# A feed-forward's last projection with Strassen's scheme on 7 of its 20 pairs of weight rows

## The chip, the cores and the metric

The kernel runs on one core of a Trainium2 chip. The core has a matrix engine (TensorE, PE in the profile; PEld is its loading of the stationary operand), a vector engine (VectorE, DVE), a scalar engine (ScalarE, ACT), a general engine (GpSimd, POOL) and an engine whose queue issues transfers here (SyncE, SP). Each engine works through its own list of instructions and waits at semaphores for the others. Data lie in SBUF (128 partitions), products in the 8 banks of PSUM (128 x 512 fp32 each).

The metric is device time in microseconds, the median of several executions. A separate profiled execution gives the trace.

## The reference

A decoder trunk of two layers for 256 tokens of width 2048, in fp32. What matters here is the feed-forward and what stands behind it:

```python
def conv_glu(x, w_gate, w_up, conv_w, w_down):
    gate = causal_dwconv(x @ w_gate, conv_w)
    return (jax.nn.silu(gate) * (x @ w_up)) @ w_down
...
        x = layer_norm(DN_ALPHA * x + h, ln1_g[i], ln1_b[i])
        f = conv_glu(x, ffn_w_gate[i], ffn_w_up[i], ffn_conv_w[i], ffn_w_down[i])
        x = layer_norm(DN_ALPHA * x + f, ln2_g[i], ln2_b[i])
        x = x + jax.nn.sigmoid(x @ ple_w_gate[i]) * (p[i] @ ple_w_proj[i])
```

`w_gate` and `w_up` are 2048 x 5120, `w_down` is 5120 x 2048. Layer 0 has a gated delta-rule mixer ahead of this, layer 1 a sparse attention.

## The kernel before

**Splitting.** A matrix product is done in fp32r on TensorE with each operand split in two: a high half (a copy into fp32r on ACT, L127) and a low half (the rest, on DVE, L128). The product is high x high, low x high and high x low, three matmuls. Activations are kept split: `hT` holds the feed-forward's inner activations, transposed, 40 blocks of 128 rows, each with a high and a low plane of 256 tokens (32 blocks in the tile hTA, 8 in hTB). Weights come from HBM into `raw` (4 buffers of 128 x 1024 fp32, issued on SP's queue, L122) and are split into `hi` and `lo` (3 buffers each, 128 x 1024).

**Gate and up.** `ffn` runs over pairs of blocks n, n+1 of the 5120 columns. `gemm_t_steps` (L160, L164) computes the gate and then the up product of a pair, transposed; `gate` applies the convolution and Silu, `up` multiplies the two and splits the result into `hT` (L941 to L943). Both read `xT`, the split transposed input, which nobody needs after the last up product until the layer norm writes it anew.

**The last projection.** `project` computes `hT` x `w_down` in four blocks of 512 columns, one after the other (`project_steps`, `gemm_steps`). A step takes two row-blocks of 128 and 512 columns of weights, one `raw` and one `hi`/`lo`, and does 12 matmuls of 512 columns: for each row-block and each half of 128 tokens, high x high (L199) and low x high (L202), then high x low for all (L206). Two PSUM banks hold the two token halves. At the end of a block `residual` adds the sum to 4^(1/4) times `x` (L263) and takes statistics (L264). That is 20 steps of 12 for each block, 960 matmuls per layer.

**The end.** In the last block the last two steps are taken together, first the whole of token half 0, then of half 1, so that the layer norm's scale of half 0 (`scale_of`, L297 to L306) is worked out while half 1 runs. `held` splits two weight tiles of the next projection ahead of time; `fetch` loads the small projection's weights into the upper half of `xT` ahead of the last block; `fill` runs that small projection (`ple_w_proj`) on TensorE while the layer norm transposes its rows (L331) and writes `xT`.

**Order.** Instructions get a priority by the order in which the code writes them; `high_priority` moves some forward, and the weights' splits stand 1000 places forward. When the program is built, each engine's list is made from these priorities and from what is ready at each point by the builder's own times; `after` pins one instruction behind another. A tile's buffer is free for the next use when its last reader has done.

**PSUM.** The tags `mm0` and `mm1` have two banks each and are taken in turn (`banks`); `sp` and `bk` have two each, for everything else.

## Time and profile before

| | us |
|---|---|
| median of 3 runs | 2766.88 |
| lowest and highest | 2762.75, 2767.78 |
| profiled execution | 2763.9 |
| its span in the profile | 2762.1 |

The profile has one row for each group of alike instructions: its line in the kernel, engine, operation, the names of the tiles (written <- read), the shape, the count; then busy time and the mean of one in ns; then the idle time of the engine ahead of it and what ended it. The view of windows gives the busy time of each engine in a stretch. The view in order of time gives start and length of each instruction or run of alike ones. Ends of matmuls are modelled and overlap the next one's start, so the spacing of the starts is what counts.

### The profile page before, as it was taken

The page shows a single profiled execution, that of the slowest core. Times are in us where ns is not written, and L with a number is a line of the kernel's source. Part 1 is how long each engine was busy: PE and PEld are TensorE (multiplying, and loading weights), DVE is VectorE, ACT ScalarE, POOL GpSimd, SP SyncE. Part 2 cuts the span into 40 slices and gives each one's busy share as a digit, 9 for nine tenths or more (in the row PEclk, how much of TensorE's full clock was granted, in tenths as well). Part 3 has the DMA queues.
Part 4 walks back from the last instruction along what each step waited for, and adds up shares of the span by engine and source line. Part 5 has one row for each costly group of instructions (what it writes and reads, how often), then busy time and mean ns, then how long its engine had stood idle before and what let it go on. Part 6 is the DMA issues. An engine that isn't in the chain of part 4 may idle for free. (4 is left out here: it accounts for less than half of the span.)

```text
span 2762.1 us, 40056 instructions
## 1 busy us (share of the span) xinstructions
PE 2735.3 (99%) x14604; PEld 2352.9 (85%) x14604; DVE 1853.0 (67%) x3109; ACT 1485.7 (54%) x2512; POOL 428.9 (16%) x834
## 2 busy tenths in 40 slices
PE   9999999999999999999999999999999999999999
PEld 7888888888888888888888888888888888888887
DVE  7877877877466666666545765765766666655566
ACT  5576666776545555555334544455455555543444
POOL 1665545665000000000000000210000000000000
PEclk9999999999999999999999999999999999999999
DMA  8776667666575666676666567545566666666655
GB/s 225 188 203 175 181 176 187 157 192 168 187 217 158 193 206 204 204 208 198 196 193 207 176 189 234 170 145 165 167 198 197 199 191 193 197 192 194 209 172 193
DMA packets 410566, 525.09 MB, mean 190 GB/s; under 512 B 24352, under 2 KB 299024, under 8 KB 410112
## 3 DMA queue, kind: packets, MB, share of 16 engines
q1 hardware_dynamic: 397872, 495.65, 59.7%
q0 software_dynamic: 12496, 26.88, 3.9%
q8 instruction: 114, 1.87, 0.3%
q14 instruction: 84, 0.69, 0.1%
HBM read 516.62 MB, written 8.97 MB: 190 GB/s over the span
## 5 line engine op out<-in xcount | busy, mean ns | idle before, releaser
L128 DVE TENSOR_TENSOR lo<-raw,hi 128x1024 fp32r<-128x1024 f32 (+1 forms) x920 | 1125.3, 1225 | 582.1 <-ACT hi L127 565.0
L127 ACT ACTIVATE hi<-raw 128x1024 fp32r<-128x1024 f32 (+1 forms) x920 | 967.1, 1053 | 664.8 <-PE mm_ps L202 415.4
L160 PE MATMUL mm_ps<-xT,hi 128*128 128x512 f32 (+1 forms) x4176 | 1031.8, 395 | 7.6 <-DVE xT L242 5.6
L160 PEld LDWEIGHTS mm_ps<-xT,hi 128*128 128x128 f32 (+1 forms) x4176 | 763.1, 189 | 154.8 <-ACT hi L241 6.1
L164 PE MATMUL mm_ps<-xT,lo 128*128 128x256 f32 (+1 forms) x4176 | 557.0, 284 | 1.7 <-DVE lo L128 1.7
L164 PEld LDWEIGHTS mm_ps<-xT,lo 128*128 128x128 f32 (+1 forms) x4176 | 538.7, 191 | 23.2 <-DVE lo L128 2.5
L199 PE MATMUL mm_ps<-hi,xT 128*128 128x512 f32 (+1 forms) x704 | 272.3, 388 | 0.0
L202 PE MATMUL mm_ps<-hi,xT 128*128 128x512 f32 (+1 forms) x704 | 269.0, 384 | 0.0
L237 ACT ACTIVATE fold<-mm_ps 128x256 f32<-128x256 f32 x261 | 98.0, 376 | 264.7 <-PE mm_ps L160 264.2
L256 POOL DMA_DIRECT2D lng<-in_ln_g x16 | 8.8, 549 | 1239.6 <-PE mm_ps L206 654.0
L202 PE MATMUL mm_ps<-hi,hTA 128*128 128x512 f32 x512 | 199.3, 389 | 0.0
L199 PE MATMUL mm_ps<-hi,hTA 128*128 128x512 f32 x512 | 199.3, 389 | 0.0
L206 PE MATMUL mm_ps<-lo,xT 128*128 128x512 f32 (+1 forms) x704 | 189.4, 384 | 0.0
L202 PEld LDWEIGHTS mm_ps<-hi,xT 128*128 128x128 f32 x704 | 132.3, 188 | 24.4
L199 PEld LDWEIGHTS mm_ps<-hi,xT 128*128 128x128 f32 x704 | 132.2, 188 | 24.1
L206 PEld LDWEIGHTS mm_ps<-lo,xT 128*128 128x128 f32 x704 | 129.8, 188 | 24.3
L206 PE MATMUL mm_ps<-lo,hTA 128*128 128x512 f32 x512 | 136.9, 389 | 0.0
L688 POOL TENSOR_TENSOR xi<-xi,xt 128x60 f32<-128x60 f32 (+24 forms) x248 | 121.2, 489 | 19.4
L686 POOL TENSOR_TENSOR xt<-ld,xi 128x60 f32<-128x60 f32 (+24 forms) x248 | 114.1, 460 | 53.4 <-DMA ld<-lt 34.6
L199 PEld LDWEIGHTS mm_ps<-hi,hTA 128*128 128x128 f32 x512 | 96.1, 188 | 20.0
L206 PEld LDWEIGHTS mm_ps<-lo,hTA 128*128 128x128 f32 x512 | 96.2, 188 | 19.9
L202 PEld LDWEIGHTS mm_ps<-hi,hTA 128*128 128x128 f32 x512 | 96.2, 188 | 19.8
(268 smaller groups left out, 2657.7 us busy)
## 6 DMA issues: line engine op xcount, KB each, us to landing
raw<-in_gdn_w_in SPq DMA_DIRECT2D x192, 512.0 KB, 4.5
raw<-in_ffn_w_gate SPq DMA_DIRECT2D x160, 512.0 KB, 4.1
raw<-in_ffn_w_up SPq DMA_DIRECT2D x160, 512.0 KB, 4.4
raw<-in_ffn_w_down SPq DMA_DIRECT2D x160, 512.0 KB, 3.8
raw<-in_dsa_w_in SPq DMA_DIRECT2D x72, 512.0 KB, 3.7
raw<-in_gdn_w_o SPq DMA_DIRECT2D x64, 512.0 KB, 4.2
raw<-in_ple_w_gate SPq DMA_DIRECT2D x64, 512.0 KB, 4.8
raw<-in_dsa_w_o SPq DMA_DIRECT2D x32, 512.0 KB, 3.8
```

Source lines behind the costliest of these rows:

```text
L127: act = nc.scalar.activation(hi, raw, AF.Copy)
L128: ins = nc.vector.tensor_tensor(lo, raw, hi.bitcast(F32), op=ALU.subtract)
L160: ins = nc.tensor.matmul(q[:m, :], hi[:, k, o:o + m], x[:, k0 + k].rearrange("p a b -> p (a b)"), start=k0 + k == 0, stop=last)
L164: ins = nc.tensor.matmul(q[:m, S:], lo[:, k, o:o + m], x[:, k0 + k, 0, :], start=False, stop=last)
L199: ins = nc.tensor.matmul(ps[a][:, :n], xh, hi, start=k == 0, stop=False)
L202: self.before = self.recent = nc.tensor.matmul(ps[a][:, :n], xl, hi, start=False, stop=False)
L206: self.last = self.recent = nc.tensor.matmul(ps[a][:, :n], x(k)[:, 0, a * P:(a + 1) * P], lo, start=False, stop=k == kt - 1)
L237: nc.scalar.activation(t[:m], ps[:, S:], AF.Copy)
L256: ins = self.nc.gpsimd.dma_start(out=r, in_=bass.AP(tensor=src.tensor, offset=src.offset, ap=[[0, P], [1, n]]))
L686: nc.gpsimd.tensor_tensor(tmp[:, :m, :w], bcast(ld[:, i + 1:, i], m, 1), xi[:, :m, i:i + 1].to_broadcast([P, m, w]), op=ALU.mult)
L688: nc.gpsimd.tensor_tensor(xi[:, :m, i + 1:], xi[:, :m, i + 1:], tmp[:, :m, :w], op=ALU.subtract)
```

## The change

Of the 20 pairs of row-blocks in `w_down` (2m and 2m+1), 7 (m = 0, 3, 6, 9, 12, 15, 18) go by Strassen's scheme. There the left operand is 2 x 2 blocks (two token halves, two row-blocks), the right one 2 x 2 (two row-blocks, two column blocks of 512), and seven products with sums of blocks as operands take the place of eight. I call these the fast pairs and the other 13 the plain ones.

- The projection now goes over two column halves of 1024. A plain pair takes two `raw` tiles, one row-block of 1024 columns each, and does 24 matmuls into four banks. A fast pair takes two such tiles as well and does 21 matmuls into seven banks.
- `pair` makes the right operands: in place in `raw`, four sums of 512 columns on DVE, and splits into two `hi`/`lo` tiles (the first block of the first row-block; both blocks of the second) and into the lower half of `xT`, planes `th` and `tl` (four sums). The order is: split of the first block, two sums, split of the second row-block, two sums, two splits into `xT`.
- The left operands come from `up`: for fast pairs it forms sums of token halves, three forms of 128 columns per pair. For the first two fast pairs they are split into the new tile `some` at once; for the other five they wait as fp32 in free parts of `pw` and are split into the upper half of `xT` just ahead of their first use.
- Three products go straight into the banks of the result (`own`), four into banks of their own (`one`, `six`, `seven`, `five`), which gather over all seven fast pairs. After the last fast pair of a column half (`j == final`) one ACT copy and eight DVE sums of 512 columns add them to `x`; the closing sum (`done`) then is one addition and the statistics for each of four blocks.
- The two column halves use the two sets of four banks in exchange.
- The last pair of the second half finishes token half 0 in two blocks of 512 columns, then half 1 in two. `fetch` comes after the last fast pair.

```diff
--- before.py
+++ after.py
@@ -915,6 +915,168 @@
         return self.layer_norm(pool, g, b, gb, copies)
 
 
+    def pair(self, src, m, c):
+
+
+        nc = self.nc
+        raw = [self.wp.tile([P, 1024], F32, tag="raw", name="raw") for _ in range(2)]
+        for k, r in enumerate(raw):
+            nc.sync.dma_start(out=r, in_=src[(2 * m + k) * P:(2 * m + k + 1) * P, c:c + 1024])
+        flat = self.xT.rearrange("p k a s -> p k (a s)")
+        th, tl = flat[:, 0:4], flat[:, 4:8]
+        (h0, l0), (h1, l1) = ((self.hl.tile([P, 1024], F32R, tag=k, name=k) for k in ("hi", "lo")) for _ in range(2))
+        (b11, b12), (b21, b22) = ((r[:, :512], r[:, 512:]) for r in raw)
+        less = lambda o, x, y: nc.vector.tensor_tensor(o, x, y, op=ALU.subtract)
+        with self.tc.high_priority(offset=W_AHEAD):
+            self.split(h0[:, :512], l0[:, :512], b11)
+            less(b11, b12, b11)
+            less(b12, b22, b12)
+            self.split(h1, l1, raw[1])
+            less(b22, b22, b11)
+            less(b21, b21, b22)
+            for i in range(2):
+                self.split(th[:, 2 * i:2 * i + 2], tl[:, 2 * i:2 * i + 2], raw[i].rearrange("p (k s) -> p k s", k=2))
+        return [(th[:, i], tl[:, i]) for i in range(4)] + [(h0[:, :512], l0[:, :512])] + [
+            (h1[:, n:n + 512], l1[:, n:n + 512]) for n in (0, 512)]
+
+    def fours(self, turn):
+
+
+        if turn:
+            return self.banks(2) + self.banks(2)
+        return [self.sp.tile([P, 512], F32, tag=tag, name="mm_ps") for tag in ("sp", "sp", "bk", "bk")]
+
+    def chunk_steps(self, src, i, h, forms, order, turn, held=None):
+
+
+        nc, c = self.nc, 1024 * i
+        forms, plain = forms
+        own = self.fours(turn)
+        one, six, seven, five = self.fours(1 - turn)
+        begun = set()
+
+        def mul(bank, x, y, stop=False):
+            ins = self.recent = nc.tensor.matmul(bank, x, y, start=id(bank) not in begun, stop=stop)
+            begun.add(id(bank))
+            return ins
+
+        xs = lambda n: [self.x[:, a, c + 512 * j:c + 512 * j + 512] for a in range(2) for j in range(2)][n]
+
+        def add(o, x, y):
+            nc.vector.tensor_tensor(o, x, y, op=ALU.add)
+
+        def plus(n, ps):
+            nc.vector.scalar_tensor_tensor(xs(n), xs(n), ALPHA, ps, op0=ALU.mult, op1=ALU.add)
+
+        def done(n):
+            add(xs(n), xs(n), own[n])
+            nc.vector.bn_stats(self.st[:, n // 2, 2 * i + n % 2], xs(n))
+
+        final = max(j for j, m in enumerate(order) if m in forms)
+        for j, m in enumerate(order):
+            end = j == len(order) - 1
+            k0, k1 = h(2 * m), h(2 * m + 1)
+            if m in forms:
+                f = forms[m]
+                if m in plain and not i:
+                    with self.tc.high_priority(offset=W_AHEAD):
+                        self.split(f[:, 0, :S], f[:, 1, :S], plain[m][0])
+                        self.split(f[:, 0, S:], f[:, 1, S:], plain[m][1])
+                t1, t3, t4, t2, b11, b21, b22 = self.pair(src, m, c)
+                items = [(one, k0[:, :, :P], b11), (own[0], k1[:, :, :P], b21), (own[1], f[:, :, :P], b22),
+                         (five, f[:, :, P:S], t1), (seven, k0[:, :, P:], t3), (six, f[:, :, S:], t2), (own[2], k1[:, :, P:], t4)]
+                for q, x, y in items:
+                    for z in range(2):
+                        mul(q, x[:, z], y[0])
+                for q, x, y in items[3:] + items[:3]:
+                    mul(q, x[:, 0], y[1], stop=j == final and any(q is y for y in (one, five, six, seven)))
+                if j == final:
+                    u = [self.pw[:, 0, k:k + 512] for k in (1024, 1536)]
+                    nc.scalar.activation(u[0], one, AF.Copy)
+                    plus(0, one)
+                    add(u[0], u[0], six)
+                    plus(1, u[0])
+                    add(u[1], u[0], seven)
+                    plus(2, u[1])
+                    plus(3, u[1])
+                    add(xs(1), xs(1), five)
+                    add(xs(3), xs(3), five)
+            else:
+                parts = [self.weights(src, (2 * m + k) * P, 1, (c, 1024)) for k in range(2)]
+                parts = [(x, hi[:, 0], lo[:, 0]) for x, (hi, lo) in zip((k0, k1), parts)]
+                if end and held is not None:
+                    held()
+                behind = self.last if end and held is not None else None
+
+                def run(a, ns, low):
+                    for j, (x, hi, lo) in enumerate(parts):
+                        x = x[:, :, a * P:(a + 1) * P]
+                        for z in range(1 if low else 2):
+                            for n in ns:
+                                ins = mul(own[2 * a + n], x[:, z], (lo if low else hi)[:, 512 * n:512 * n + 512],
+                                          stop=bool(end and low and j == 1))
+                                if behind is not None:
+                                    self.after(ins, behind)
+                    return ins
+
+                if not end:
+                    for low in range(2):
+                        for a in range(2):
+                            self.last = run(a, (0, 1), low)
+                else:
+                    for a in range(2):
+                        for ns in ((0,), (1,)) if held is not None else ((0, 1),):
+                            self.before = run(a, ns, 0)
+                            self.last = run(a, ns, 1)
+                            for n in ns:
+                                done(2 * a + n)
+                        if held is not None:
+                            self.scales.append(self.scale_of(self.norm, self.st, a))
+            yield
+
+    def project_pairs(self, pool, src, h, forms, g, b, cols, prepare, lead):
+
+        nc = self.nc
+        self.st = pool.tile([P, 2, 4, 6], F32, tag="st", name="st")
+        self.norm, self.scales = pool, []
+        quick = list(forms[0])
+        slow = [m for m in range(self.PAIRS) if m not in quick]
+        order = slow[:1]
+        rest = slow[1:]
+        for j, m in enumerate(quick):
+            n = 1 + (j % 2 == 0)
+            order += rest[:n] + [m]
+            rest = rest[n:]
+        self.go_(self.chunk_steps(src, 0, h, forms, order + rest, 0))
+        gb = pool.tile([P, 2 * KT], F32, tag="gb", name="gb")
+        nc.gpsimd.dma_start(out=gb, in_=cols)
+        fetch, fill = prepare()
+
+        def held():
+            for x in lead:
+                self.early(*x)
+
+        order = slow[:2]
+        rest = slow[2:]
+        for m in quick:
+            order += [m] + rest[:1]
+            rest = rest[1:]
+        order += rest
+        last = self.chunk_steps(src, 1, h, forms, order, 1, held=held)
+        for j in range(len(order) - 1):
+            next(last)
+            if order[j] == quick[-1]:
+                fetch()
+        with self.tc.high_priority():
+            self.go_(last)
+        late = self.split_by
+        with self.tc.high_priority():
+            copies = fill()[-2:]
+        self.split_by = late
+        return self.layer_norm(pool, g, b, gb, copies)
+
+    QUICK, PAIRS = (0, 3, 6, 9, 12, 15, 18), 20
+
     def ffn(self, i, affine):
         nc, tc, t = self.nc, self.tc, self.t
         with tc.tile_pool(name="hp", bufs=1) as hp, tc.tile_pool(name="fp", bufs=1) as pool:
@@ -936,11 +1098,40 @@
                                                    op0=ALU.mult, op1=ALU.add)
                 self.mark = nc.scalar.activation(ac, ac, AF.Silu)
 
+            quick = self.QUICK
+            some = pool.tile([P, 2, 2, 3 * P], F32R, tag="some", name="some")
+            xf, rf = (y.rearrange(z) for y, z in ((self.xT, "p k a s -> p (k a s)"), (self.pw, "p a d -> p (a d)")))
+            forms, plain = {}, {}
+            for j, m in enumerate(quick):
+                forms[m] = some[:, j] if j < 2 else xf[:, 4096 + 768 * (j - 2):4096 + 768 * (j - 1)].rearrange(
+                    "p (a s) -> p a s", a=2)
+                if j >= 2:
+                    c0, c1 = ((1024, 1280), (1408, 1664), (3072, 3328), (3456, 3712), (1792, 3840))[j - 2]
+                    plain[m] = rf[:, c0:c0 + S], rf[:, c1:c1 + P]
+            raws = {}
+
             def up(n, ps):
-                h = pool.tile([P, S], F32, tag="fh", name="fh", bufs=2)
+                h = raws[n] = pool.tile([P, S], F32, tag="fh", name="fh", bufs=2)
                 self.fold(pool, h, ps)
                 nc.vector.tensor_tensor(h, h, gates[n], op=ALU.mult)
-                self.split(hT(n)[:, 0], hT(n)[:, 1], h)
+                if n // 2 not in quick:
+                    self.split(hT(n)[:, 0], hT(n)[:, 1], h)
+                elif n % 2:
+                    one, f = raws[n - 1], forms[n // 2]
+                    self.split(hT(n)[:, 0], hT(n)[:, 1], h)
+                    nc.vector.tensor_tensor(h[:, P:], h[:, P:], one[:, P:], op=ALU.add)
+                    nc.vector.tensor_tensor(one[:, P:], one[:, :P], one[:, P:], op=ALU.subtract)
+                    self.split(hT(n - 1)[:, 0], hT(n - 1)[:, 1], one)
+                    s = plain.get(n // 2)
+                    last = s[1] if s else one[:, :P]
+                    nc.vector.tensor_tensor(last, h[:, P:], one[:, :P], op=ALU.subtract)
+                    if s:
+                        nc.scalar.activation(s[0][:, P:], h[:, P:], AF.Copy)
+                        nc.vector.tensor_tensor(s[0][:, :P], h[:, :P], last, op=ALU.subtract)
+                    else:
+                        nc.vector.tensor_tensor(h[:, :P], h[:, :P], last, op=ALU.subtract)
+                        self.split(f[:, 0, :S], f[:, 1, :S], h)
+                        self.split(f[:, 0, S:], f[:, 1, S:], last)
 
             distances = self.distances(pool) if not i else iter(())
             for n in range(0, NF, 2):
@@ -955,8 +1146,8 @@
                     next(distances, None)
                 if n in (6, 14, 22, 30):
                     affine(pool, n // 8, self.mark)()
-            return self.project(pool, t["ffn_w_down"][i], hT, NF, t["ln2_g"][i], t["ln2_b"][i], t["ln2_t"][i], lambda: self.fill,
-                                [(t["ple_w_gate"][i], 0, 2, (c, 512)) for c in (0, 512)])
+            return self.project_pairs(pool, t["ffn_w_down"][i], hT, (forms, plain), t["ln2_g"][i], t["ln2_b"][i], t["ln2_t"][i],
+                                      lambda: self.fill, [(t["ple_w_gate"][i], 0, 2, (c, 512)) for c in (0, 512)])
 
 
     def lead(self, i):
```

## The prediction

> **What bounds the kernel now.** I read the page's first and second parts, then the windows view of the two stretches in which the changed projection runs, then the waits of TensorE.
>
> ```profile
> span 2762.1 us, 40056 instructions
> PE 2735.3 (99%) x14604; PEld 2352.9 (85%) x14604; DVE 1853.0 (67%) x3109; ACT 1485.7 (54%) x2512; POOL 428.9 (16%) x834
> 846.00:1300.00 454.00, 453.38 (x2593) 398.64 (x2592) 306.70 (x454) 247.57 (x378) 9.48 (x17) 1.00 0.66 196
> 1308.64:1517.00 208.36, 208.36 (x921) 172.66 (x920) 106.19 (x97) 84.93 (x83) 0.00 (x0) 1.00 0.62 200
> 2453.00:2659.15 206.15, 206.15 (x911) 170.81 (x910) 103.96 (x96) 80.36 (x76) 0.00 (x0) 1.00 0.62 199
> ```
>
> TensorE (PE) is busy 2735.3 of 2762.1 us. The second and third window rows are the last feed-forward projection of the two layers: PE has no gap in them at all, VectorE (DVE) is busy 106.19 of 208.36 us, ScalarE (ACT) 84.93, and the granted clock is 1.00. So here time is the number of matmuls times their spacing, and DVE has about 100 us per layer to give away. The first window row is a layer's gate and up projections: DVE 306.70 of 454 us, PE 453.38.
>
> ```profile
> 1351.47 1.07 PE L206 MATMUL mm_ps<-lo,hTA 128*128 128x512 f32 x4
> 1351.67 1.06 ACT L127 ACTIVATE hi<-raw 128x1024 fp32r<-128x1024 f32 x1 [1.66 <-PE mm_ps L202]
> 1352.38 0.39 PE L199 MATMUL mm_ps<-hi,hTB 128*128 128x512 f32 x1
> 1352.77 1.23 DVE L128 TENSOR_TENSOR lo<-raw,hi 128x1024 fp32r<-128x1024 f32 x1 [1.49 <-ACT hi L127]
> 1354.19 1.07 PE L206 MATMUL mm_ps<-lo,hTB 128*128 128x512 f32 x4
> 1354.39 1.06 ACT L127 ACTIVATE hi<-raw 128x1024 fp32r<-128x1024 f32 x1 [1.66 <-PE mm_ps L202]
> 1355.10 0.39 PE L199 MATMUL mm_ps<-hi,hTB 128*128 128x512 f32 x1
> ```
>
> This is one step of the projection in order of time. From 1352.38 to 1355.10 are 12 matmuls in 2.72 us: **0.2267 us each**. A matmul's row lasts 0.39 us, so its result is there about 0.16 us after the next has begun. ACT writes a high half (1.06 us) as soon as TensorE has done with the buffer, DVE the low half 0.04 us later (1.23 us). The buffers, three of each half, decide when a split may start: this matters below.
>
> **What the change removes.** A plain pair of weight rows takes, per 1024 columns, 8 block products of 3 matmuls, 24 in all; a fast pair 7 of 3, 21. There are 7 fast pairs, 2 column halves and 2 layers: 28 fast pairs, 84 matmuls fewer, 84 x 0.2267 = **-19.0 us**. PE has no gap there, so all of it would show if nothing else came to wait. The Trainium skill ("TensorE: Matmul & The Clock Gate", section "Part 2: What happens when you issue a matmul") gives a sustained spacing of about 131 ns for 512 columns in a real kernel; by that 84 matmuls would be 11.0 us. The rows above show 226.7 ns here, and the sum goes by them.
>
> **What it adds on DVE.**
>
> ```profile
> L128 DVE TENSOR_TENSOR lo<-raw,hi 128x1024 fp32r<-128x1024 f32 x904 | 1111.9, 1231 | 573.9 <-ACT hi L127 559.4 <-PE mm_ps L206 7.5 <-PE l_ps L770 2.1
> L1010 DVE TENSOR_TENSOR x<-x,sg 128x512 f32<-128x512 f32 x16 | 10.8, 688 | 0.3
> L263 DVE SCALAR_TENSOR_TENSOR x<-x,mm_ps 128x512 f32<-128x512 f32 x32 | 21.6, 682 | 5.2 <-PE mm_ps L206 5.2
> L264 DVE BATCH_NORM_STATS2 st<-x 128x6 f32<-128x512 f32 x32 | 21.9, 690 | 0.5
> L494 DVE SCALAR_TENSOR_TENSOR v<-v,ac 128x128 f32<-128x128 f32 x64 | 19.5, 329 | 0.5 <-ACT v L493 0.5
> L242 DVE TENSOR_TENSOR hTA<-fh,hTA 128x256 fp32r<-128x256 f32 x64 | 26.8, 422 | 14.8 <-ACT hTA L241 14.5
> ```
>
> A sum of 512 fp32 columns is 0.69 us (L1010; 0.68 with one operand in PSUM, L263), a low half of 1024 columns 1.23. A plain pair stays at 2 x 1.23 = 2.46 us. A fast pair has one low half of 512, four sums of 512 and three low halves of 1024: 5 x 0.69 + 3 x 1.23 = **7.14 us**, against 21 x 0.2267 = 4.76 us of PE. Where one fast and one plain pair alternate (the second column half), that is 9.60 us of DVE in 45 x 0.2267 = 10.20 us of PE: 94%. Each column half ends its fast pairs with eight sums out of PSUM, 8 x 0.69 = 5.5 us. The four closing sums with their statistics (4 x 1.38 = 5.5 us per half) replace four of L263 and L264, so they are not new. In the up projection a fast pair adds four sums of 128 columns at 0.33 (L494), 1.3 us, and split forms of 256 and 128 columns, 0.42 + 0.33, there or just ahead of their use: at most 7 x 2.1 = 15 us per layer, beside a stage where DVE idles 147 of 454 us (first window row). I cost it at nothing; only if that cover went would some of 15 us show. Weight DMAs keep their number and size (80 of 512 KB per layer); only their rows grow longer.
>
> **What comes to wait.** The new operand forms make a chain, and it begins late. Each row-block takes a high and a low buffer out of three. A fast pair's second row-block gets its low buffer when the pair before has done with its first: at matmul 22 of 24. Let 0 be the moment at which the fast pair may start. That matmul starts 3 x 0.2267 = 0.68 earlier and ends 0.39 later: -0.29. Then, in order: 0.04, low half 1.23, the sum for the third operand 0.69, for the fourth 0.69 (these two overwrite the rows that the low half reads, so they can't go first), 0.04, ACT's high half 1.06, 0.04. The third and fourth forms are ready at **+3.50**. As written TensorE wants them after 10 matmuls, at +2.27: a wait of **1.23 us per fast pair**, more than the 0.68 that it saves. In strict order of writing, 28 x 1.23 = 34.4 us.
>
> But the order on an engine isn't that of writing. Look at the start of a layer's gating, where the code has L199, L202, L199, L202:
>
> ```profile
> 2666.24 0.44 PE L331 MATMUL n_ps<-ident,x 128*128 128x128 f32 x2 [0.45 <-ACT x L319]
> 2666.43 0.71 PE L199 MATMUL mm_ps<-hi,xT 128*128 128x512 f32 x2
> 2666.99 0.63 PE L202 MATMUL mm_ps<-hi,xT 128*128 128x512 f32 x2
> 2667.45 0.39 PE L199 MATMUL mm_ps<-hi,xT 128*128 128x512 f32 x1
> PE n_ps L331 <- ACT x L319: 1.8, 4, 0.4
> ```
>
> Two of L199 stand together, then two of L202: what was ready when the program was put in order went ahead of what wasn't. In the same way the wait can be filled: the three low products of the first, second and third operand (0.68 us), then high products of the next pair on other banks. How well such an order, fixed beforehand, meets the chip shows in the last rows: PE still waits 0.45 us at 2666.24, and 1.8 us in 4 waits of this kind. So the rest per fast pair lies between 0 and 1.23; nearest is this row with 0.45 at its most, and I take 0.20, as three to five fillers of 0.23 are there: 28 x 0.20 = **+5.6**.
>
> Behind the blocked low half DVE's queue holds the next pairs' low halves, and behind those wait TensorE and the raw buffers. From the end of the first half's fast pairs to the last fast pair of the second half DVE has 9 plain and 7 fast pairs, eight sums and the closing: 22.1 + 50.0 + 5.5 + 5.5 = 83.1 us, PE 9 x 5.44 + 7 x 4.76 = 82.3. That is 0.8 us too much. Within the alternation there is a loop as well, through the raw buffer:
>
> ```profile
> raw<-in_ffn_w_down SPq DMA_DIRECT2D x160, 512.0 KB, 3.8
> L1008 ACT ACTIVATE sg<-mm_ps 128x512 f32<-128x512 f32 x16 | 9.5, 592 | 21.5 <-PE mm_ps L206 11.0 <-DVE x L1010 10.4
> ```
>
> landing 3.8, high half 0.59 (as L1008) and 0.08 of handing on, low half 0.69, two sums 1.38, the other low half 1.23, two sums 1.38, and the low half that frees the raw rows 1.23: 10.38 us against PE's 10.20, 7 x 0.18 = 1.3 us. Together 2.1, I take 2.0 per layer: **+4.0** (each layer 0, if it runs ahead far enough, to 5.5, if all eight sums come in front).
>
> **The end of each projection.** The last pair finishes a token half in two blocks of 512 where there was one, so two more DVE operations (0.68 and 0.69) lie among the small ones of the layer norm's scale. There PE had 0.45 to wait already (2666.24), so between 0 and 1.38 us per layer; I take half: **+1.4**. It can't be a gain: the block that starts the scale ends where it did.
>
> **Operands in other places.** Four of seven products now stream from xT, 28 x 4 x 3 = 336 matmuls.
>
> ```profile
> 1290.32 3.82 PE L160 MATMUL mm_ps<-xT,hi 128*128 128x512 f32 x16
> 851.91 0.40 PE L199 MATMUL mm_ps<-xT,pT 128*128 128x512 f32 x1
> 852.15 0.39 PE L202 MATMUL mm_ps<-xT,pT 128*128 128x512 f32 x1
> ```
>
> Streaming from xT the up projection takes (3.82 - 0.39) / 15 = 0.2287, and the small projection at 851.91 0.24. That is 0.002 to 0.013 more each, 0.7 to 4.4 us. I take the longer row's 0.7: **+0.7**.
>
> **Sum:** -19.0 + 5.6 + 4.0 + 1.4 + 0.7 = **-7.3 us**. The profiled execution took 2763.9 us (span 2762.1 and 1.8 around it): 2756.6. The median of the runs before is 2766.88, 3.0 above the profiled one; on it the forecast is **2759.6 us**.
>
> **Rivals.**
>
> 1. *All of it is filled.* The order leaves no rest at the forms, and DVE, with about half its time free before, runs ahead in the first half, where two plain pairs often stand between fast ones. For it: the projection had not one PE gap. What stays is 1.4 + 0.7: -16.9, **2750.0**. A row that speaks for it comes from the first stage of the kernel:
>
> ```profile
> 69.00:138.00 69.00, 69.00 (x354) 59.10 (x354) 58.19 (x125) 40.44 (x75) 44.89 (x89) 1.00 0.75 188
> 345.00:414.00 69.00, 66.42 (x382) 57.72 (x381) 54.29 (x135) 46.24 (x109) 31.65 (x67) 1.00 0.67 175
> ```
>
> With DVE busy 58.19 of 69 us PE lost nothing; but with 54.29 of 69 it lost 2.58 elsewhere.
>
> 2. *Slower: the wait at the third form stays.* One mechanism at one place: the low buffer of the second row-block comes at -0.29 and the form at +3.50, and TensorE's order holds the third form's products ahead of enough fillers, because the order was made with shorter times than DVE's 1.23 and 0.69. It decides from 0.68 us per fast pair on: there the wait eats the three saved matmuls. At its full 1.23: -19.0 + 34.4 + 1.4 + 0.7 = +17.5, **2784.4**. The raw loop has slack then and adds nothing.
>
> 3. *DVE becomes the bound in the second half.* 83.1 against 82.3 us leaves no room; if the eight sums go in front of the splits (5.5 per layer) and the fast pairs' rest is 0.25: -19.0 + 7.0 + 11.0 + 1.4 + 0.7 = +1.1, **2768.0**.
>
> That the change doesn't drop the products can be excluded from its code: each fast pair issues seven times three.
>
> **How the numbers follow.** Forecast 0.42, the first rival 0.26, the second 0.20, the third 0.12. A measurement of this kernel can tell about 0.2%, 5.5 us, from no change. The forecast's own range is -12 to -2 us (2755 to 2765), 0.27 of its 0.42 beyond -5.5. So faster 0.27 + 0.26 = 0.53; same 0.15 and 0.10 of the third, 0.25; slower 0.20 + 0.02 = 0.22. The predicted time is the forecast's, 2759.6. At its lower end the range takes in the whole 19.0 (2747.9, say 2748); at the upper end it takes in the third rival and a third of the second one, whose time lies anywhere from +5.5 to +17.5: 2776. About 0.16 is left out.
>
> **What would show it.** PE has 84 rows fewer, 14604 - 84 = 14520; the projection's stretch has 918 matmuls and lasts 918 x 0.2267 = 208.1 us per layer plus its waits. The view of PE's waits names the third and fourth forms' high half (the split written into xT) or the low halves: under 0.3 us each by the forecast, near 1.2 with 28 of them by the second rival, none by the first. DVE is busy about 190 of some 210 us there. In time order, fillers (low products of the first three operands, or high products of the next pair) stand ahead of the third form's. I am wrong if the waits sit at PSUM banks at the change of column halves, if spacing differs from 0.2267 in the fast pairs, or if the up projection gains PE gaps.

## The result, and the profile after

| | before | after |
|---|---|---|
| median, us | 2767.33 (4 runs) | 2782.57 (4 runs) |
| lowest and highest | 2762.75, 2768.84 | 2779.55, 2785.76 |
| span of the profiled execution | 2762.1 | 2777.7 |

The ratio of after to before is 1.0058, with an interval of 1.0039 to 1.0077: the change makes the kernel slower by some 15 us, where 7.3 us less was forecast. The profiled execution after is the one of 2779.55 us.

From the page of after, its span, its first part and its row of weight loads (KB of each, median us from issue to landing):

```profile
span 2777.7 us, 40310 instructions
...
PE 2736.8 (99%) x14520; PEld 2334.1 (84%) x14520; DVE 2006.3 (72%) x3393; ACT 1538.8 (55%) x2610; POOL 430.7 (16%) x834
...
raw<-in_ffn_w_down SPq DMA_DIRECT2D x160, 512.0 KB, 4.8
```

The products are gone as counted (14604 - 84 = 14520 matmuls), yet TensorE is busy no less. A load of the projection's weights lands in 4.8 us (median), 3.8 before.

The view of windows of after, the columns being PE, PEld, DVE, ACT and POOL busy, granted clock, DMA share and GB/s: the two projections whole, from their first matmul to the first of the small projection, then the first one in four parts (first column half, change of halves, the alternating fast and plain pairs of the second half, and its end).

```profile
1311.38:1536.26 224.88, 218.53 (x920) 170.42 (x919) 177.48 (x207) 108.22 (x117) 0.00 (x0) 0.99 0.58 191
2451.31:2674.76 223.45, 217.00 (x919) 170.67 (x918) 177.29 (x207) 108.19 (x117) 0.00 (x0) 0.99 0.60 193
...
1311.30:1417.70 106.40, 106.40 (x461) 85.43 (x460) 81.92 (x96) 53.54 (x60) 0.00 (x0) 1.00 0.58 188
1417.70:1427.20 9.50, 7.64 (x31) 5.36 (x31) 8.47 (x13) 2.77 (x3) 0.00 (x0) 1.00 0.66 232
1427.20:1503.00 75.80, 73.53 (x305) 55.09 (x303) 62.65 (x71) 39.12 (x43) 0.00 (x0) 1.00 0.52 173
1503.00:1536.20 33.20, 30.97 (x127) 24.57 (x127) 24.47 (x29) 12.86 (x13) 0.00 (x0) 0.95 0.73 231
```

A projection lasts 224.88 and 223.45 us; before it was 217.60 in both layers. 918 matmuls at 0.2267 are 208.1, so 16.8 and 15.4 us are lost, where before nothing was. The first half loses 106.40 - 461 x 0.2267 = 1.9 us, the change of halves 9.50 - 31 x 0.2267 = 2.5, the alternation 75.80 - 305 x 0.2267 = 6.7, the end 33.20 - 127 x 0.2267 = 4.4, at a clock of 0.95. (At their edges these windows count six matmuls more than 918, which is the 1.4 us that the four losses are short of 16.8.) Both projections together are 13.1 us longer than before. Of the 15.6 by which the span grew the other 2.5 lie ahead of 766 us of the trace, in the first layer's mixer, where no line was changed. That stretch differs by more between executions with the same code there: the first projection starts between 1308.15 and 1312.69 us in e9 to e12 below. So these 2.5 us say nothing of the change.

The waits of PEld and of PE in after, in all, how many and the longest (us):

```profile
PEld mm_ps L959 <- ACT xT L241: 17.4, 31, 2.5
PEld mm_ps L959 <- DVE xT L242: 8.7, 20, 0.7
PEld mm_ps L959 <- ACT hi L127: 3.1, 5, 1.4
PEld mm_ps L959 <- DVE x L966: 2.6, 2, 1.3
...
PE n_ps L331 <- ACT x L319: 1.8, 4, 0.4
```

Most waits, 51 of them, sit at the forms written into xT. The last row, the layer norm's start, is what it was before.

Now after in order of time, first in the alternation, then at the last fast pair:

```profile
1452.63 0.69 DVE L929 TENSOR_TENSOR raw<-raw 128x512 f32<-128x512 f32 x1 [1.24 <-DMA raw<-in_ffn_w_down]
...
1456.95 1.22 DVE L128 TENSOR_TENSOR lo<-raw,hi 128x1024 fp32r<-128x1024 f32 x1
1458.09 0.69 DVE L929 TENSOR_TENSOR raw<-raw 128x512 f32<-128x512 f32 x1
1458.69 1.22 DVE L128 TENSOR_TENSOR lo<-raw,hi 128x1024 fp32r<-128x1024 f32 x1
1459.83 0.68 DVE L929 TENSOR_TENSOR raw<-raw 128x512 f32<-128x512 f32 x1
1460.55 1.06 ACT L241 ACTIVATE xT<-raw 128x1024 fp32r<-128x1024 f32 x1 [4.00 <-DVE raw L929]
1461.66 0.73 PE L959 MATMUL mm_ps<-xT 128*128 128x512 f32 x2 [0.63 <-ACT xT L241]
...
1467.68 0.69 DVE L929 TENSOR_TENSOR raw<-raw 128x512 f32<-128x512 f32 x1
1468.28 1.22 DVE L128 TENSOR_TENSOR lo<-raw,hi 128x1024 fp32r<-128x1024 f32 x1
1468.43 1.43 SPq L924 DMA_DIRECT2D raw<-in_ffn_w_down  x2
...
1475.56 0.69 DVE L929 TENSOR_TENSOR raw<-raw 128x512 f32<-128x512 f32 x1 [1.33 <-DMA raw<-in_ffn_w_down]
...
1501.45 1.06 ACT L127 ACTIVATE xT<-raw 128x1024 fp32r<-128x1024 f32 x1 [0.24 <-DMA raw<-in_ple_w_proj]
1503.37 0.68 DVE L929 TENSOR_TENSOR raw<-raw 128x512 f32<-128x512 f32 x1
1504.15 1.06 ACT L241 ACTIVATE xT<-raw 128x1024 fp32r<-128x1024 f32 x1 [0.79 <-DVE raw L929]
1505.26 0.72 PE L959 MATMUL mm_ps<-xT 128*128 128x512 f32 x2 [2.06 <-ACT xT L241]
```

Four things are to be seen. First, DVE's list has two low halves of the plain pair (1456.95, 1458.69) ahead of and between the third and the fourth sum, so that ACT waits 4.00 us for these sums and TensorE 0.63 for ACT. Second, at 1452.63 and again two alternations later, at 1475.56, a fast pair's second sum waits for its raw rows to land: one alternation takes (1475.56 - 1452.63) / 2 = **11.46 us** here, where its 45 matmuls need 10.20 (from the first to the last fast pair of the second half the mean is 11.3 us in the first layer, 11.1 in the second). Third, the two loads for the pair at 1475.56 are issued late (SPq L924, 1468.43, two in one row). The first follows a third sum (1467.68 + 0.69), which was the last to read its tile. The second, for which the sum at 1475.56 waits, is issued at 1469.53, as soon as a low half of the plain pair (1468.28 + 1.22) frees the next tile, and lands 5.9 us later. Fourth, at the last fast pair a split of the small projection's weights (L127 at 1501.45, which `fetch` brought) stands in ACT's list ahead of the last forms, and TensorE waits 2.06 us.

### The profile page after: what moved, and what is told of

It reads as the page before. It is cut to its first block, busy times and chain, and to the rows that moved or that the text cites. A ratio compares the mean times of both kernels' runs of the same rounds, so it can differ in the third digit from the quotient of the medians.

```text
span 2777.7 us, 40310 instructions
## 1 busy us (share of the span) xinstructions
PE 2736.8 (99%) x14520; PEld 2334.1 (84%) x14520; DVE 2006.3 (72%) x3393; ACT 1538.8 (55%) x2610; POOL 430.7 (16%) x834
## 5 line engine op out<-in xcount | busy, mean ns | idle before, releaser
L128 DVE TENSOR_TENSOR lo<-raw,hi 128x1024 fp32r<-128x1024 f32 (+1 forms) x864 | 1055.4, 1224 | 407.0 <-ACT hi L127 379.3
L127 ACT ACTIVATE hi<-raw 128x1024 fp32r<-128x1024 f32 (+1 forms) x864 | 906.1, 1052 | 495.7 <-PE mm_ps L202 174.1
L959 PE MATMUL mm_ps<-hi,hTA 128*128 128x512 f32 x736 | 188.4, 393 | 4.3 <-DVE x L966 1.8
L959 PEld LDWEIGHTS mm_ps<-hi,hTA 128*128 128x128 f32 x736 | 138.1, 189 | 38.4 <-ACT hi L127 3.1
L199 PE MATMUL mm_ps<-hi,oT 128*128 128x512 f32 x256 | 101.6, 397 | 0.5 <-ACT hi L127 0.5
L959 PE MATMUL mm_ps<-lo,hTA 128*128 128x512 f32 x368 | 99.8, 391 | 0.5 <-DVE lo L242 0.5
L202 PE MATMUL mm_ps<-hi,oT 128*128 128x512 f32 x256 | 100.2, 391 | 0.0
L489 DVE SCALAR_TENSOR_TENSOR ac<-pd,cw,ac 128x256 f32<-128x256 f32 x192 | 95.2, 505 | 4.5 <-ACT ac L487 3.2
```

Source lines behind the costliest of these rows:

```text
L127: act = nc.scalar.activation(hi, raw, AF.Copy)
L128: ins = nc.vector.tensor_tensor(lo, raw, hi.bitcast(F32), op=ALU.subtract)
L199: ins = nc.tensor.matmul(ps[a][:, :n], xh, hi, start=k == 0, stop=False)
L202: self.before = self.recent = nc.tensor.matmul(ps[a][:, :n], xl, hi, start=False, stop=False)
L489: nc.vector.scalar_tensor_tensor(ac, pd[:, k:k + S], w[:, k:k + 1], ac, op0=ALU.mult, op1=ALU.add)
L959: ins = self.recent = nc.tensor.matmul(bank, x, y, start=id(bank) not in begun, stop=stop)
```

## The experiments

Four theories of the loss. The expectations number them:

1. **Rows held.** The in-place sums keep the raw tiles in use, one until the third sum and the other until the pair's last split, so the next loads are issued late and land late.
2. **Forms late.** The third and fourth form stand behind the low buffer of the second row-block, as in the prediction's second rival.
3. **Load.** DVE has too much to do in the alternation.
4. **Order.** The plain pair's low halves inside the chain of sums delay it.

Below, "a layer's length" is that of the projection as above, first and second layer. The runs came in sets, each with the kernel before beside it: 2776.79 us (e1 to e4), 2776.76 (e5 to e8), 2764.1 (e9 to e12), 2779.18 (e13), 2776.2 (e14 to e16). So times are compared within a set, and lengths across them. The times of e1 to e10 and of e14 to e16 are single executions, and each length is that of one profiled execution. The same kernel (e7 and e11) differs by 1.0 and 2.0 us in length, so differences of that size tell nothing. Diffs are against after unless another kernel is named.

| kernel | time, us | a layer's length | lost beside 208.1 |
|---|---|---|---|
| after | 2782.57 | 224.88, 223.45 | 16.8, 15.4 |
| e1, no sums | 2766.26 | 210.10, 209.25 | 2.0, 1.2 |
| e2, rows apart | 2826.41 | 243.96, 242.63 | 35.9, 34.5 |
| e3, sums elsewhere | 2770.74 | 212.73, 215.83 | 4.6, 7.7 |
| e4, fetch later | 2783.47 | 222.41, 220.46 | 14.3, 12.4 |
| e5, sums in a row | 2817.94 | 236.91, 234.50 | 28.8, 26.4 |
| e7, own tiles, fetch later | 2765.07 | 211.81, 209.51 | 3.7, 1.4 |
| e8, the same, spaced | 2771.20 | 212.36, 212.26 | 4.3, 4.2 |
| e9, low half first | 2788.49 | 228.30, 228.62 | 20.2, 20.5 |
| e10, rows held | 2750.72 | 211.14, 211.84 | 3.1, 3.8 |
| e11, as e7 | 2752.34 | 210.80, 211.49 | 2.7, 3.4 |
| e12, closing sums ahead | 2752.29 | 211.41, 210.09 | 3.3, 2.0 |
| e13, rows kept long | 2781.08 | 219.26, 222.97 | 11.2, 14.9 |
| e14, forms late | 2779.00 | 215.65, 214.64 | 7.6, 6.6 |
| e15, rows kept shorter | 2778.00 | 222.26, 220.77 | 14.2, 12.7 |
| e16, forms later | 2773.05 | 214.86, 215.42 | 6.8, 7.3 |

### e1: without the four sums

```diff
-            less(b11, b12, b11)
-            less(b12, b22, b12)
             self.split(h1, l1, raw[1])
-            less(b22, b22, b11)
-            less(b21, b21, b22)
```

> Leaves out the four 512-column sums that form the right operands (products run on unsummed rows); every split, every matmul and the closing sums stay. This asks what the sums and the chain through them cost in all. The projection took 217.6 us per layer before and takes 224.9 and 223.5 with the change; 918 matmuls at 0.2267 are 208.1. If the loss (16.8 and 15.4 us) comes from the chain of sums or from DVE's load, the second column half loses at most 2 us in place of 6 to 7 and a layer's projection takes 211 to 214 us, the whole about 2759 us. If the loss comes from the restructuring itself (two column halves, seven banks, matmuls that stream from xT), it stays above 220 us per layer.

Measured: 2766.26 us, 10.5 less than the kernel before in its set, and 2.0 and 1.2 us lost. So 918 matmuls do take some 208 us, in another order, with other operands and seven banks; the sums are the price, by themselves or by what they hold up.

### e2: the fast pairs' raw rows in tiles of their own

```diff
-        raw = [self.wp.tile([P, 1024], F32, tag="raw", name="raw") for _ in range(2)]
+        raw = [self.pw[:, k, :1024] for k in range(2)]
```

These rows lie over half of the small projection's product, which is lost.

> The fast pairs' two row tiles lie in a free part of pw, so the plain pairs have the four raw buffers alone: six in all. Theory 1 (the raw rows of a fast pair are held until the last form is split, and the 4.8 us landing of the next then closes a loop of 11.4 us against 10.2 of TensorE): the second half's loss of 7.1 and 6.1 us falls to 2 to 3, a projection takes 219 to 221 us, the whole falls by 7 to 10 us. Theory 2 (the low buffer of the second row-block comes too late) and theory 3 (DVE's load of 94 per cent): no change, within 1 us per layer.

Measured: far slower (of the 70 us lost 15 go by the clock, see the last section). It was a poor test: with two tiles of their own instead of two out of four the fast pairs' loads wait for the fast pair before. SP's queue waits 169.8 us in 24 waits for its sums (9.3 the longest). It shows what late rows can do, not what the changed kernel loses by them.

### e3: the last two sums out of place, ahead of the low half

```diff
+            away = self.pw[:, 0, :1024]
+            less(away[:, 512:], b22, b11)
+            less(away[:, :512], b21, away[:, 512:])
             self.split(h1, l1, raw[1])
-            less(b22, b22, b11)
-            less(b21, b21, b22)
...
+            for i, r in enumerate((raw[0], away)):
```

The two sums lie over part of the small projection's product, which is lost.

> The last two sums are written to a free part of pw and not over the rows that the low half reads, and the low half of the second row-block comes after them: the third form no longer waits for a low buffer. Theory 2: the waits for the form's high half (31 on TensorE's weight loads, 17.4 us) mostly go, the first half's loss falls from 2.1 and 2.7 us to under 1, the second's from 7 to 3 or 4; the whole falls by 8 to 12 us. Theory 1: the first half stays as it is, the second gains what is cut from the loop (1.2 us of 11.4), some 3 us per layer. Theory 3: no change, since DVE does the same work.

Measured: 4.6 and 7.7 us lost, 12.2 and 7.7 fewer than in after, and no wait at a form in the first half; over 2 us of the rest is a wait in each layer behind the last fast pair (in the second layer 1.7 more go by the clock). Once the sums no longer overwrite what the low half reads, they need not wait for it, and the rows are free sooner too. This tells the place of the loss, not which of theories 1 and 2 it is.

### e4: the small projection's weights fetched two pairs later

```diff
-            if order[j] == quick[-1]:
+            if j == order.index(quick[-1]) + 2:
                 fetch()
```

> The small projection's weights are fetched and split two plain pairs later. With the change the last fast pair of each layer waits 2.50 us for its third form, with two of those splits ahead of the two last sums on DVE and ACT, and the clock is 0.95 after it. If the fetch is the cause: that wait falls to that of the other fast pairs, about 1 us, the clock stays at 1.00, the tail's loss of 4.6 and 4.9 us falls to 1.5 to 2.5 and the whole falls by 5 to 7 us. If the last fast pair is late for another reason (DVE behind, raw rows late), nothing changes.

Measured: 2.5 and 3.0 us per layer less; the longest wait at a form falls from 2.5 to 1.1 us. The early fetch adds 5.5 us in all to what the sums cost, 3.4 of them by the clock (last section). It costs only together with the sums: e1 fetches as early and loses 0.1 us from its last fast pair on.

### e5: the plain low halves behind the sums

```diff
+            self.sums = less(b21, b21, b22)
...
+                    parts.append(self.weights(src, (2 * m + k) * P, 1, (c, 1024)))
+                    if self.sums is not None:
+                        self.after(self.split_by[1], self.sums)
```

> Only the order of DVE's list changes: the plain pair's two low halves are pinned behind the fast pair's last sum. In the changed kernel's list they stand one between the second row-block's low half and the third sum, one between the third and the fourth (2 x 1.23 us inside the chain). Theory 4 (the chain is late because of these two): with the buffers and DVE's work as they were, the projection falls from 224.9 and 223.5 us to 213 to 217, as in the run with the sums elsewhere. Theory 2 (the low buffer comes too late): the chain still starts 0.29 us ahead of the fast pair, the third form still 3.5 us into it; the first half's loss stays above 1.5 us, the projection above 219. Theory 1 (raw rows, landing 4.8 us): the last split comes 2.5 us sooner, so the second half gains too, 217 to 220.

Measured: 11 to 12 us per layer worse than after. ACT's group of the first forms, in after and then in e5 (busy us, mean ns | idle ahead of it and what ended it):

```profile
L241 ACT ACTIVATE hi<-raw 128x512 fp32r<-128x512 f32 (+1 forms) x58 | 48.4, 838 | 69.6 <-DMA raw<-in_ffn_w_down 35.5 <-PE mm_ps L959 32.0 <-DVE raw L929 1.7
```
```profile
L241 ACT ACTIVATE hi<-raw 128x512 fp32r<-128x512 f32 (+1 forms) x58 | 48.4, 837 | 110.2 <-DMA raw<-in_ffn_w_down 82.0 <-PE mm_ps L959 26.7 <-DVE raw L929 1.4
```

With the chain in one piece ACT's idle time ahead of these splits that ended with a load rose from 35.5 to 82.0 us: the plain pair's low halves came later, its rows with them, and so the next fast pair's rows. The row speaks for theory 1. Theory 4 finds no support, but it is hardly tested: the high halves of the third and fourth form came 6.0 us after the pair's first matmul (median of 28 pairs), only 0.4 sooner than in after (6.4).

### e6, e7, e11: the last two sums in tiles of their own

```diff
+            a22, a21 = (self.norm.tile([P, 512], F32, tag="xb", name="away", bufs=2) for _ in range(2))
+            less(a22, b22, b11)
+            less(a21, b21, a22)
             self.split(h1, l1, raw[1])
-            less(b22, b22, b11)
-            less(b21, b21, b22)
-            for i in range(2):
-                self.split(th[:, 2 * i:2 * i + 2], ...)
+            self.split(th[:, :2], tl[:, :2], raw[0].rearrange("p (k s) -> p k s", k=2))
+            self.split(th[:, 3], tl[:, 3], a22)
+            self.split(th[:, 2], tl[:, 2], a21)
```

The tiles are two that the layer norm uses only later. e7 has e4's later fetch as well; e11 is e7 in five rounds.

> As the run with the sums elsewhere, but with the two last sums in two idle tiles of 512 columns (those of the layer norm) and four splits for the forms in place of three: 0.15 us more DVE per fast pair. Theory 2: 212 to 216 us per layer, no waits at the forms in the first half. It leaves the whole at about 0 to -4 us against the kernel before.

> The same and the small projection's weights two plain pairs later. With the sums elsewhere, TensorE waited 2.07 and 2.23 us for a plain pair's high half right behind the last fast pair, which stands behind those splits on ACT. If the fetch holds it, these waits go: 210 to 213.5 us per layer, 2 to 3 less than without. If not, no change.

> The version with own tiles and later fetch again, in rounds: 11.7 us (0.42 per cent) below the kernel before in its single look; its projections take 5.8 and 8.1 us less than 217.6, so 10 to 14 us less than before, ratio 0.995 to 0.9965.

Measured: from e6 no time can be taken: its one execution took 9697.87 us, at a mean granted clock of 0.473. e7 took 2765.07 us against 2776.76. e11 took 2752.34 (2748.49 to 2755.51 in 6 runs) against 2764.1 (11 runs): a ratio of 0.9955, interval 0.994 to 0.997. **This version beats both kernels.** From e11, the windows of the two projections, and in order of time one fast pair of the alternation:

```profile
1312.69:1523.49 210.80, 209.84 (x919) 171.76 (x918) 178.59 (x221) 106.35 (x131) 0.00 (x0) 1.00 0.63 204
2438.19:2649.68 211.49, 209.53 (x920) 171.76 (x918) 178.51 (x221) 106.25 (x131) 0.00 (x0) 1.00 0.62 204
...
1447.40 0.68 DVE L929 TENSOR_TENSOR away<-raw 128x512 f32<-128x512 f32 x1
1448.12 0.69 DVE L929 TENSOR_TENSOR away<-raw,away 128x512 f32<-128x512 f32 x1
1449.25 1.13 ACT L241 ACTIVATE xT<-away 128x512 fp32r<-128x512 f32 x2
1449.81 1.07 PE L961 MATMUL mm_ps<-hi,hTA 128*128 128x512 f32 x4
1450.52 1.22 DVE L242 TENSOR_TENSOR lo<-raw,hi 128x1024 fp32r<-128x1024 f32 x1
...
1452.07 0.62 PE L961 MATMUL mm_ps<-xT 128*128 128x512 f32 x2
```

The last two sums (1447.40, 1448.12) now come some 2 us ahead of the pair's first matmul (1449.81), and ahead of its low half (1450.52), and the forms are there before TensorE wants them, at 1452.07. DVE is busy 178.59 us, no less than in after, in a stretch 14 us shorter (12 in the second layer).

### e8: the second half spaced as the first

On e6's kernel:

```diff
-        for m in quick:
-            order += [m] + rest[:1]
+        for j, m in enumerate(quick):
+            n = 1 + (j % 2 == 1)
+            order += [m] + rest[:n]
...
-            if order[j] == quick[-1]:
+            if j == order.index(quick[-1]) + 1:
```

> The same (fetch one plain pair behind the last fast one), and in the second half one and two plain pairs stand in turn between fast ones, as in the first half, two and not five behind the last. If what is left in the second half is DVE's load of 94 per cent in strict alternation (theory 3) or the raw loop (theory 1), its loss falls to that of the first half, under 1 us: 209 to 211.5 us per layer. If what is left sits at the change of halves, nothing falls; if the two remaining plain pairs are too few to hide the eight closing sums, the end grows by 1 to 4 us.

Measured: 4.3 and 4.2 us lost, no fewer than in e7. From the first to the last fast pair of the second half, where DVE has the relief, it is 1.1 and 1.4, in e7 1.2 and 0.9; what it loses more than e7 lies behind the last fast pair, where the fetch comes one pair sooner than in e7. Relief for DVE wins nothing here: theory 3 finds no support.

### e9: the low half first, the sums out of place

On e7:

```diff
-            less(a22, b22, b11)
+            _, low = self.split(h1, l1, raw[1])
+            self.after(less(a22, b22, b11), low)
             less(a21, b21, a22)
```

> The version with own tiles and later fetch, one thing put back: the third sum is pinned behind the second row-block's low half, which waits for its buffer until 0.29 us ahead of the fast pair. The raw rows are freed no later than the last sum. Theory 2 (the late low buffer): the chain is 3.5 us late again, the loss of 3.7 and 1.4 us rises to 8 or more, 216 to 222 us per layer, and TensorE waits at the forms' high halves in the first half too. Theory 1 (the raw rows held too long): within 2 us of the version without, 210 to 214.

Measured: 228.30 and 228.62 us, 17.5 and 17.1 more than e11. So the place of these sums behind that low half is the root of most of the loss. But the sums also read the raw rows, which now come free 4.4 us after the pair's first matmul and not 1.9, so this doesn't yet tell theory 2 from theory 1.

### e10: the rows held by the low half

On e7, with the low half of the second row-block behind all splits of the forms:

```diff
-            self.split(h1, l1, raw[1])
+            nc.scalar.activation(h1, raw[1], AF.Copy)
...
+            _, low = self.split(th[:, 2], tl[:, 2], a21)
+            self.after(nc.vector.tensor_tensor(l1, raw[1], h1.bitcast(F32), op=ALU.subtract), low)
```

> The same version with the other thing put back: the sums still go ahead and don't wait for a low buffer, but the second row-block's low half, the last reader of its raw rows, is pinned behind all splits of the forms, so those rows are freed as late as with the change. Theory 1: the loss rises, to 218 us or more per layer, with waits of ACT for the raw rows' landing in the second half. Theory 2: no wait at the forms, 210 to 214 us.

Measured: 211.14 and 211.84, 0.35 more than e11 in each layer. Read alone, this fells theory 1. The trace shows why it may not: the low half was pinned late but ran only 1.2 us later in the first half and 2.2 in the second (medians), and the second tile was free 3.1 and 4.0 us after the pair's first matmul, where in after it is 7.7 (pair at 1354.23, last split over at 1361.94).

### e12: the eight closing sums ahead

On e7, with the nine operations after `if j == final:` inside `high_priority(offset=W_AHEAD)`.

> The same with the eight closing sums of a column half put as far forward in DVE's order as the weights' splits. At the change of halves TensorE waited 0.6 us for a closing sum and 0.6 to 0.8 us for the next fast pair's form behind them. If the low priority of those sums causes the rest of the loss: 1 to 2 us per layer less than without, ratio about 0.9945. If they push the splits back instead, the loss moves to the next fast pair and nothing is won.

Measured: 2752.29 us (5 runs), a ratio of 0.9954 (0.9939 to 0.9969): the same as e11. In front of the splits, as the prediction's third rival has them, the closing sums cost nothing here.

### e13 and e15: the rows held, the forms not pinned

On e7, one more reader of the second raw tile, behind the second (e13) or the first (e15) low half of the plain pair that follows:

```diff
+                        keep = self.norm.tile([P, 1], F32, tag="keep", name="keep", bufs=2)
+                        self.after(nc.vector.tensor_copy(keep, self.kept[:, :1]), self.split_by[1])
```

> The kernel with sums in their own tiles and the later fetch, in which each fast pair's second raw tile gets one more reader: DVE copies one column of it, pinned behind the low half of the second row-block of the plain pair that follows. Nothing that the forms need waits for it. So the rows are held to about 5.8 us after the start of the fast pair, against 1.9 without that, 4.4 in the kernel where the third sum stands behind the low half, and 7.7 in the changed kernel. Theory 1 (rows held too long make the next loads late, and that is the price): the projection lasts 222 to 230 us per layer, and ScalarE waits for the loads as in the kernel with the pinned third sum (over 60 us in all). Theory 2 (the low buffer makes the forms themselves late): it stays at 211 to 213 us per layer, TensorE's waits at the forms written into xT under 5 us in all, and the execution is within 3 us of the same kernel without the extra reader. In between (214 to 221) both have a part, and the share is what it shows.

> As the kernel with rows kept long, but the extra reader of the second raw tile is pinned behind the first low half of the following plain pair, so the rows are held to about 4.2 us after the pair's start, where the kernel with the pinned third sum held them 4.4. Theory 1 with a gradual price: between 211 and the 219 to 223 of the longer hold, 214 to 217 us per layer. Theory 1 with a loop that has slack up to there: 211 to 212, and then the held rows do not explain the kernel with the pinned third sum. Theory 2 says 211 to 212 too.

Measured: e13 219.26 and 222.97, e15 222.26 and 220.77. Against the mean of e7 and e11 (211.3 and 210.5) that is 20 us (1.7 of them by the clock, see the last section) and 21 us for the two layers together: as much as the sums cost in place, and no less with the shorter hold. ACT's group of the first forms in e15:

```profile
L241 ACT ACTIVATE hi<-raw 128x512 fp32r<-128x512 f32 (+1 forms) x58 | 48.6, 838 | 131.7 <-DMA raw<-in_ffn_w_down 97.1 <-PE mm_ps L962 24.5 <-DVE lo L128 5.9
```

97.1 us of its idle time ended with a load (26.7 in e11). Theory 1 holds: held rows alone can make a loss of this size. The holds came out longer than expected: the second tile was free 4.5 us after the pair's first matmul in the first half and 6.5 in the second in e15, 5.9 and 7.0 in e13 (medians). Held to 3.1 and 4.0, in e10, the rows cost next to nothing. The forms are late here too, though nothing pins them, since their rows land late; TensorE waits most for their low halves, in e15:

```profile
PEld mm_ps L962 <- DVE xT L242: 13.8, 29, 0.9
```

One side effect stands beside the hold: in 12 of the 28 pairs DVE's list has the second row-block's low half ahead of the first forms' (4 of 28 in e11). e16 below has it in 10, with the rows free early, and loses no more than e14.

### e14 and e16: the forms late, the rows free

On e7, one column (e14) or all (e16) of the two sums copied onto itself, behind the low half:

```diff
+            _, low = self.split(h1, l1, raw[1])
+            for k in (a22, a21):
+                self.after(nc.vector.tensor_copy(k[:, :1], k[:, :1]), low)
```

> The kernel with sums in their own tiles and the later fetch; the two sums read the raw rows early as there, but DVE then copies one column of each sum onto itself, pinned behind the low half of the second row-block, so that the two forms wait for the late low buffer again while the raw rows come free as early as before (1.9 us after the pair's start). The forms are then ready about 3 us after the start, 0.7 behind where TensorE wants them in strict order. Theory 2 (late forms alone make the loss): some 28 x 0.3 to 0.7 us, 215 to 220 us per layer. Theory 1 (held rows make it): 211 to 212 us per layer.

> As the kernel with late forms, with the whole 512 columns of each sum copied onto itself (0.69 us or less each), so the forms come at the times of the chain in the prediction, up to 3.5 us after the pair's start, with the raw rows free early. It adds at most 1.4 us of DVE per fast pair, some 19 of 211 us per layer. Theory 2: 28 x up to 1.2 us, 220 us or more per layer. Theory 1: at most 213 us per layer; the prediction's fillers then cover the chain, and what it cost came by the raw rows.

Measured: 215.65 and 214.64, 214.86 and 215.42: in both some 8.5 us more than e7 and e11, that is 8.5 / 28 = 0.30 us per fast pair. The high halves of the two forms came 2.6 and 3.1 us after the pair's first matmul in e14, 2.9 and 3.4 in e16 (medians), near the +3.50 of the prediction's chain. The waits of PEld in e14:

```profile
PEld mm_ps L963 <- ACT xT L241: 18.0, 39, 1.4
```

Theory 2 has a part of its own, a smaller one. In e16 DVE is busy 186.6 us of 214.86, 8 more than in e11, without more loss than in e14: theory 3 falls.

In after these forms come later still, at 6.4 us. In the first column half that costs no more: from its first to its last fast pair after loses 2.0 and 2.7 us in the two layers, e14 2.0 and 2.2, e16 2.3 and 2.3. Over the same stretch of the second half, where fast and plain pairs alternate, after loses 6.7 and 5.3, e14 4.5 and 3.2, e16 3.5 and 4.0, e15 8.7 and 7.7, e11 1.1 and 1.3. What forms as late as in after would cost there with the rows free was not tried.

**What the runs leave.** Per execution, from the lengths: 84 products -19.0 us; the sums in place +21.6 (e4 against e7: 10.6 and 10.95); the early fetch +5.5 (after against e4); what e7 still loses +5.1; together +13.2 against the 13.1 by which the projections grew. That this comes out is no proof: each term is the difference of two lengths. Within the 21.6, held rows alone make 20 to 21 and late forms alone 8.5; they overlap. How they divide where both act stays open. The length of the hold does not order the losses: e9, with both causes and the rows free after 4.4 us, lost 34.6 us more than e11, more than the two alone, and after, with 7.7 us, fewer. Why was not tried.

## Why the prediction was wrong

- **What bounds the kernel, and -19.0: right.** PE has 84 matmuls fewer, and in e1 the two projections are 15.9 us shorter than before. The new operands and orders stream no slower (16 matmuls in 3.79 us from 1348.79, as before), so the +0.7 for other places is not to be seen.
- **DVE's work: right in size, and no bound.** Sums of 0.69 and low halves of 1.22 us were measured; busy 177 us per layer against 190 forecast.
- **The rest at the third form, +5.6: right in kind, somewhat small.** TensorE's order has the fillers that the prediction reckoned with (low products of the first operands, then the plain pair's high ones). With the rows free, forms about as late as the reckoned +3.50 cost 0.30 us a pair (e14, e16), 8.5 in all; 0.20 was taken. The chain itself was too short: in after the low half that begins it starts 0.6 us after the pair's first matmul and not at -0.29, two low halves of the plain pair stand in it, and the high half is ready at 6.4 us.
- **The loop through the raw rows, inside +4.0: this is the step that failed.** The prediction wrote 10.38 us against 10.20, so 1.3 us per layer. It named the right loop, but took its landing of 3.8 from the kernel before and left out the plain pair's two low halves, which stand inside the chain in DVE's list. In after the first load of a fast pair still lands in 3.7 us, but the second in 5.4 (medians of 28), and the second sum needs both. Measured were 11.46 us per alternation in the two shown, 11.3 and 11.1 in the mean of six, 6.7 and 5.3 us lost there in the two layers; held rows alone cost 10 us per layer (e13, e15). How much of it is the landing and how much the low halves was not separated. A loop with a margin of 0.18 us was priced as if it had only one possible value. The page of the kernel before showed landings of 3.7 to 4.8 us for loads of 512 KB, by tensor, and both ends belonged into its bounds.
- **DVE's balance of 83.1 against 82.3 us, the other part of +4.0: wrong.** In the kernels with the sums out of place, the closing sums ahead (e12), wider spacing (e8) and 8 us more of DVE (e16) change nothing.
- **The end of each projection, +1.4: 0.** The layer norm's wait at L331 is 1.8 us in 4 waits before and after.
- **A term that was missing: the moved `fetch`, 5.5 us.** The prediction didn't count the two splits that it brings and their low halves, which stand ahead of the last forms.
- **The second rival's 2784.4 lies near the measured 2782.57, yet not by its mechanism.** It charged 34.4 us to forms that are ready at +3.50; forms about that late cost 8.5 by themselves. It also held that the raw loop has slack when forms are late; in after the two come together. Its place was right, in-place sums that stand behind a late low half; that its price came so near to the measured time is luck.

## What to carry to other kernels

Where a scheme makes sums of operands, write the sums out of place, into tiles that idle at that time, so that neither the forms nor the release of the loaded rows wait for a split whose buffer is recycled late; here that and a later fetch turned 0.6% slower into 0.45% faster. Price a loop through a load by the longest landing and by everything that the engine's list puts between landing and release, and treat a margin of 2% as none. When an experiment is meant to delay something, read in its trace by how much it did so, before a theory falls by it.

## What the runs showed of the hardware

A wait of 2 us on TensorE can cost nearly as much again. From the windows of after behind the wait that ended at 1505.26 (PE busy, granted clock, DMA share, GB/s):

```profile
1505.00:1506.00 1.00, 0.74 (x3) 1.00 0.67 238
1506.00:1507.00 1.00, 1.00 (x3) 0.56 0.70 229
1507.00:1508.00 1.00, 1.00 (x4) 0.50 0.64 188
1508.00:1509.00 1.00, 1.00 (x4) 0.50 0.84 246
1509.00:1510.00 1.00, 1.00 (x5) 0.73 0.79 250
1510.00:1511.00 1.00, 1.00 (x6) 1.00 0.72 197
```

From about 1506.1 the clock is 0.50 and at 1510 it is whole again: 0.44 + 0.50 + 0.50 + 0.27 = 1.7 us lost behind a wait of 2.06. The trace's record of the clock has it at 0.50 for 3.41 us. The second layer's last fast pair has the same wait (2.07 us) and loses the same (mean 0.85 and 0.73 over two stretches of 4 us), and so does a wait of 2.05 in e13 (0.78 and 0.88 over two of 5 us). Shorter waits, 0.88 us and less at the change of halves in after, leave the clock at 1.00. But not every wait of that length costs: in e5 the last fast pair waits 2.04 us in both layers, and the clock stays at 1.00 both times. The Trainium skill ("TensorE: Matmul & The Clock Gate", section "Part 1: The HAM clock gate (the "warmup" mystery)") states that the gate passes either the whole clock or half of it and that a window of about 3.4 us decides; half a clock for 3.4 us is 1.7 us, which agrees. It puts the fall to the half behind about 3.4 us of idleness, and here 2.05 to 2.07 us were enough three times. Whole and half are not the only values that a trace shows: in e6 the granted clock is 1.00 for the first 2481 us, then 0.26 for 4.8 ms and 0.36 for 2.4. What set it so low is not known.

The same 512 KB of weights land in 3.8 us before and in 4.6 to 5.3 in the kernels behind the change (medians), which load rows of 1024 columns, at uneven times. The trace of after shows which of the two makes it: its loads land in 3.6 us where no other on the queue is under way (32 loads), in 4.8 behind one (53), 5.1 behind two (64) and 5.4 behind three (11). Of the 53, the 28 that were issued within 1.5 us of the one ahead take 5.2 to 5.4, the 12 that were issued over 3.2 us behind it 3.6. So the longer rows alone make no load late; loads that wait for their tiles and then go out close together land later. Before, they go out 2.7 us apart.
